# S5 tables, sample step and S5 scan in one row across the borders of the segments, in a hybrid decoder step on Trainium2

## The chip, the cores and the metric

One core of one Trainium2 chip runs the whole program. The metric is device microseconds from start to end of one execution; lower is better. Times before are the median of three runs. The profile is of one further execution.

## What is computed

One layer of a decoder for one prompt of 2048 tokens (width 1024) and 8 sample tokens: a mixer of mLSTM heads, S5 groups and gated-DeltaNet heads, then cross-attention and a SwiGLU FFN. Cut to the part around the change:

```
def mixer_block(x, state, lp):
    z = (rmsnorm(x, lp['norm_mix']) @ lp['w_in']).astype(f32)
    a_q, a_k, a_v, a_o, a_i, a_f, s_u, c_qkv, c_g, c_b, c_a = jnp.split(z, IN_SPLITS, axis=-1)
    ha, c1, n1, m1 = mlstm_chunked(q, k, v, a_i + ..., a_f + ..., c0, n0, m0)
    ys, s5r1, s5i1 = s5_scan(s_u.reshape(B, S, S5_GROUPS, S5_P), s5r0, s5i0, ...)
    gy = jax.nn.gelu(ys.reshape(B, S, S5_WIDTH))
    ys = gy * jax.nn.sigmoid(gy @ lp['s5_w_glu'].astype(f32))
    ...
    hc, S1 = gdn_chunked(gq, gk, gv, beta, log_alpha, S0)
    mix = jnp.concatenate([ha, ys, hc], axis=-1).astype(x.dtype)
    return x + mix @ lp['w_out'], (...)
```

`s5_scan` is a complex diagonal recurrence for 32 groups of 16 channels and 64 states. The kernel turns it into products with matrices built from the powers of each state's factor: that is what its S5 tables are.

## The kernel before

The prompt is cut into four segments of 512 tokens, `sg[0]` to `sg[3]`; the 8 sample tokens ride with the first. `win(s)` (from L443) is the input projection of one segment: 18 GEMMs of 128 output columns over the tokens, each over 8 blocks of the inner dimension with three matmuls a block (the product of two fp32 numbers by their split halves: wh times xh, wh times xl, wl times xh), and then a token-major part with three weights. For `sg[0]` a GEMM has two blocks of columns, 264 and 256. Each result is multiplied by R, the tokens' norm factor spread over the partitions (`norm_b`, copied from PSUM at L384), into a `t` tile on DVE (L152 and L155, the evacuation), and written to DRAM. Between the GEMMs of win(0) stand the 16 memory tiles (`mem_tile`, 256 columns, for the keys and values of cross-attention); between those of win(1) and win(2) eight `fold` steps each. `post(i)` is the rest of a segment: the S5 gate, output projection, cross-attention, FFN.

Weights in win(0) to win(2) come raw: SP loads `wr` (L321, ring of three), ACT casts it to `wh` (L296), POOL subtracts to get `wl` (L152), PE uses both. Raw weights are loaded and split up to two ahead. Rings that matter: `t` five tiles (`tt()`), `acc` one (`acct()`), `big` three, `x` eight, PSUM `P` four and `M` four.

Behind the GEMMs run generators that hold the rest of the mixer: `s5_tables` (from L990), `gates` and `gdn`, `mlstm`, `sample` (from L1382, the sample tokens' step), `s5` (from L1276, the scan, two halves of the prompt). `start(g, rate)` puts one in the list `bg`, `tick(w)` advances each by its rate times w steps (0.5 or 1 per GEMM), `drain` runs it to its end on the spot, `delay(n)` is n empty steps. Before, the tables are drained between win(0) and win(1), the sample step between win(1) and win(2), and scan half 0 at GEMM 17 of win(3). The order on each engine, then, is that of a scheduler that simulates the program written in this order; weights and evacuations have a priority over the generators.

Places that the change touches: `win_sq` (from L419) loads the tokens row by row into eight `t` tiles for a segment (`t<-in_xtok`, L428) and squares them on ACT (L429, sum into `rsq`); `win_rs` makes the norm factor of that with POW on POOL. `s5_tables` has two POW of 48 columns on POOL (L1007), complex powers (E) with temporaries in `t` tiles, sixteen pairs of transposes and small matmuls (L1253, and L164 with `big` and `t` as operands, in the loop over `g0`) whose inputs `bload` takes from DRAM tile T into `t` tiles (`t<-T`). In DVE's rows L1181 is the start of the E powers. `gyd` is the DRAM buffer between the scan, which writes it (L1345), and post, which reads it (`gy_load`, L1691) into a `t` tile for the gate (L1726). 

The table steps and the generator's loop that matter most:

```
        for g0 in range(0, 32, 4):
            nb_ = bload(g0 + 4) if g0 < 28 else None
            ...
                    PE.transpose(P[:, gi * 128:gi * 128 + 128], x, ident)
                    mm(P[:, 256 + gi * 16:272 + gi * 16], x, CC[:, g0 + 2 * hh + gi, :])
```

Of the kernel before, what the change touches and what calls it, by code (L numbers as in the profile page):

```python
# [66 lines left out]
def build(ctx, tc, I, O):  # L67
# [140 lines left out]
    gyd = dtile([2, 512, 8, 128], "gyd")  # L208
# [29 lines left out]
    bg = []  # L238
# [164 lines left out]
    pre = {}  # L403
# [15 lines left out]
    def win_sq(s):  # L419
# [10 lines left out]
        p["col"] = col  # L430

# [313 lines left out]
    def gdn_batch(c0, n):  # L745
# [109 lines left out]
        for j in range(n):  # L855
# [17 lines left out]
            yield  # L873
        nl = n * 16
# [115 lines left out]
    def s5_tables():  # L990
# [11 lines left out]
        def pexp(out, x):  # L1002
# [4 lines left out]
            TT(G, out, eb, x, POW)  # L1007
# [138 lines left out]
        for q0 in (0, 8):  # L1146
            SY.dma_start(pb[0], I["s5b"][:, 0, q0:q0 + 8, :])
            SY.dma_start(pb[1], I["s5b"][:, 1, q0:q0 + 8, :])
            yield from delay(2)
# [24 lines left out]
            yield from delay(2)  # L1174
# [8 lines left out]
            while m < 16:  # L1183
                x1 = tt()[:, 0:8 * m].rearrange("p (q c) -> p q c", q=8)
                x2 = tt()[:, 0:8 * m].rearrange("p (q c) -> p q c", q=8)
# [8 lines left out]
            for a0, an in ((1, 1), (2, 2), (4, 3)):  # L1194
                x1 = tt()[:, 0:8 * an].rearrange("p (q c) -> p q c", q=8)
                x2 = tt()[:, 0:8 * an].rearrange("p (q c) -> p q c", q=8)
# [32 lines left out]
        for a in range(4):  # L1229
            SY.dma_start(t5[a, :, 0:7, :], z[:, 0:7, :])  # L1230
        bb = bt()
# [5 lines left out]

        def bload(g0):
            b = tt()[:, 0:512].rearrange("p (g c) -> p g c", g=4)
            SY.dma_start(b, T1[g0:g0 + 4].rearrange("g n c -> n g c"))  # L1240
            return b

        b = bload(0)
        TS(V, CC[64:128], CC[64:128], -1.0, MUL)
# [20 lines left out]
        for l in range(8):  # L1265
            SY.dma_start(T5[:, :, 7 + l, :].rearrange("g p c -> p g c"), GG[16 * l:16 * l + 16])
        yield
# [8 lines left out]
    def s5(hf):  # L1276
# [50 lines left out]
        def st_b(g, ut, tb, mc, ms, Py):  # L1327
# [15 lines left out]
            for gi in range(2):  # L1343
                f0 = (g - 1 + gi) * 16
                SY.dma_start(gyd[hf, f0:f0 + 16].rearrange("p t c -> t p c"), q[:, gi, :])  # L1345
# [342 lines left out]
    def gy_load(s, i, T):  # L1688
        g_ = tt()
        c0 = (s.i % 2) * 64  # L1690
        SY.dma_start(g_[:, 0:512].rearrange("p (t c) -> p t c", t=8), gyd[s.i // 2, i * 128:(i + 1) * 128, :, c0:c0 + 64])  # L1691
# [359 lines left out]

    def chain(*gs):
        for g in gs:
            yield from g
# [4 lines left out]
    def win_during(s, n0=8, n1=11):  # L2059
        def f(n):  # L2060
            if n == n0:
                win_load(s)
            if n == n1:
                win_sq(s)
            if n == n1 + 2:
# [29 lines left out]
    f1 = win_during(sg[1], 3, 13)  # L2095
    win(sg[0], win0_during, win_after(sg[1]))
    drain(tabs)
    gA = start(chain(gates(0, 4), gdn(sg[0])), RT[1])
    mA = start(chain(delay(3), mlstm(sg[0])), RT[2])
    smp = start(chain(delay(1), sample()), RT[3])  # L2100
# [9 lines left out]
    drain(smp)  # L2110
    s5a = start(s5(0), RT[4])
    win(sg[2], win_fold(8, win_during(sg[3])), win_after(sg[3]))

    def pre0_during(n):
        if n == 17:
# [3 lines left out]
            drain(gA, mA, s5a)  # L2119
# [39 lines left out]
RT = [3.1, 1.6, 0.624, 1.767, 1.05, 1.092, 0.359, 0.972, 0.42, 1.1, 0.4, 1.1, 0.37]  # L2159
# [159 lines left out]
```

## Time and profile before

| | |
|---|---|
| median of 3 runs | 3242.23 us (3241.91 to 3251.68) |
| the profiled execution | 3239.78 us |
| its span, first to last instruction | 3238.0 us |
| busy: PE, DVE, ACT, POOL | 94%, 60%, 27%, 24% of the span |
| mean granted clock of TensorE | 0.973 |
| win(0) from 0, win(1) from 277, win(2) from 470, win(3) from 654, post 0 from 813 us | |

An instruction's row gives its line, engine and operation, the tile it writes and those it reads; L12 is line 12 of the kernel before. A line of a helper (L152, L155 and L164 are the helpers for elementwise work and for matmuls) covers many places, so that tiles tell which. A wait's row says who waited, for whom, and for how long in all.

### The profile page before, as it was taken

The page shows a single profiled execution, that of the slowest core. Times are in us where ns is not written, and L with a number is a line of the kernel's source. Part 1 is how long each engine was busy: PE and PEld are TensorE (multiplying, and loading weights), DVE is VectorE, ACT ScalarE, POOL GpSimd, SP SyncE. Part 2 cuts the span into 40 slices and gives each one's busy share as a digit, 9 for nine tenths or more (in the row PEclk, how much of TensorE's full clock was granted, in tenths as well). Part 3 has the DMA queues.
Part 4 walks back from the last instruction along what each step waited for, and adds up shares of the span by engine and source line. Part 5 has one row for each costly group of instructions (what it writes and reads, how often), then busy time and mean ns, then how long its engine had stood idle before and what let it go on. Part 6 is the DMA issues. An engine that isn't in the chain of part 4 may idle for free.

```text
span 3238.0 us, 49043 instructions
## 1 busy us (share of the span) xinstructions
PE 3045.7 (94%) x18185; PEld 2604.6 (80%) x18185; DVE 1933.2 (60%) x4313; ACT 867.9 (27%) x1761; POOL 772.4 (24%) x572
## 2 busy tenths in 40 slices
PE   7768889999889999999999999999999999999998
PEld 6768768778877777787799999978787787888886
DVE  8744675785789789667755665556445445332224
ACT  3124443532543232234221211132111112210001
POOL 5433545543354444431201100000000000000000
PEclk9888999999999999999999999999999999999999
DMA  7789666766778879786565665665556558455554
GB/s 230 208 205 245 199 197 215 233 205 172 266 244 301 306 260 330 265 283 235 196 211 188 208 220 181 196 236 183 178 177 199 184 174 262 159 195 185 192 183 155
DMA packets 440590, 701.16 MB, mean 217 GB/s; under 512 B 167556, under 2 KB 267628, under 8 KB 440320
## 3 DMA queue, kind: packets, MB, share of 16 engines
q1 hardware_dynamic: 401792, 673.79, 64.4%
q10 hardware_dynamic: 38560, 24.24, 2.8%
q8 instruction: 144, 2.36, 0.3%
q14 instruction: 94, 0.77, 0.1%
HBM read 533.92 MB, written 168.18 MB: 217 GB/s over the span
## 4 chain that ended last, share of the span: by engine, by line
PE 70%; DVE 13%; DMA 8%; issue 5%; POOL 2%; ACT 1%; SPq 1%; ACTq 0%; POOLq 0%; DVEq 0%
PE P L164 62%; PE M L164 7%; DVE big L152 3%; DVE t L155 2%; POOL wl L152 1%; DVE s5h L155 1%; DMA TB<-big 1%; DVE t L152 1%; DVE x L152 1%; DVE TB L152 1%; DMA t<-in_xtok 1%; DMA ABd<-AW 1%; DMA wr<-in_wmq 1%; DVE H L155 0%; DVE x L155 0%
## 5 line engine op out<-in xcount | busy, mean ns | idle before, releaser
L164 PE MATMUL P<-H,wh 128*128 128x512 f32 (+2 forms) x8032 | 2178.4, 359 | 60.4 <-DVE t L152 18.9
L164 PEld LDWEIGHTS P<-H,wh 128*128 128x128 f32 x8032 | 1415.8, 191 | 285.3 <-issue 17.0
L164 PE MATMUL P<-H,wl 128*128 128x512 f32 (+2 forms) x4016 | 1429.7, 357 | 13.1 <-POOL wl L152 12.2
L164 PEld LDWEIGHTS P<-H,wl 128*128 128x128 f32 x4016 | 765.4, 191 | 127.8 <-POOL wl L152 15.4
L152 POOL TENSOR_TENSOR wl<-wr,wh 128x1024 fp32r<-128x1024 f32 (+3 forms) x225 | 541.4, 2411 | 641.4 <-ACT wh L296 560.2
L296 ACT CAST wh<-wr 128x1024 fp32r<-128x1024 f32 (+3 forms) x227 | 231.0, 1021 | 389.7 <-PE P L164 208.9
L152 DVE TENSOR_TENSOR x<-x,P 128x512 f32<-128x512 f32 (+2 forms) x312 | 182.1, 589 | 247.8 <-PE P L164 246.2
L152 DVE TENSOR_TENSOR big<-big,big 32x60 f32<-32x60 f32 (+16 forms) x512 | 238.8, 467 | 29.5 <-DMA big<-ABd 20.5
L164 PE MATMUL P<-wh,H 128*128 128x256 f32 (+1 forms) x1280 | 241.5, 287 | 7.1 <-ACT pp L1799 3.8
L152 DVE TENSOR_TENSOR t<-P,R 128x512 f32<-128x512 f32 (+3 forms) x190 | 115.7, 614 | 218.3 <-PE P L164 180.9
L164 PEld LDWEIGHTS P<-wh,H 128*128 128x128 f32 x1280 | 202.1, 191 | 10.9 <-ACT pp L1799 7.5
L1681 ACT CAST H<-t 128x512 fp32r<-128x512 f32 (+1 forms) x120 | 73.5, 621 | 508.2 <-DVE t L152 491.9
L152 POOL TENSOR_TENSOR rs<-rcol,mhalf 128x4 f32<-128x4 f32 (+2 forms) x17 | 18.8, 1103 | 743.1 <-DVE rcol L161 734.4
L155 DVE SCALAR_TENSOR_TENSOR t<-P,R 128x512 f32<-128x512 f32 (+1 forms) x120 | 69.9, 583 | 210.7 <-PE P L164 206.7
L164 PE MATMUL P<-wl,H 128*128 128x256 f32 (+1 forms) x640 | 181.9, 285 | 1.1 <-DMA wl<-ws_A 0.7
L155 DVE SCALAR_TENSOR_TENSOR t<-t,t 128x512 f32<-128x512 f32 (+3 forms) x140 | 106.4, 765 | 67.1 <-ACT t L1912 41.6
L152 DVE TENSOR_TENSOR H<-t,H 128x512 fp32r<-128x512 f32 (+1 forms) x120 | 90.6, 764 | 64.6 <-ACT H L1681 64.4
L1912 ACT ACTIVATE t<-t 128x512 f32<-128x512 f32 (+1 forms) x88 | 55.7, 633 | 270.7 <-DVE t L152 270.5
L164 PEld LDWEIGHTS P<-wl,H 128*128 128x128 f32 x640 | 122.0, 191 | 2.4 <-DMA wl<-ws_A 1.0
L152 POOL TENSOR_TENSOR ms<-gs,TB 128x128 f32<-128x128 f32 x64 | 32.1, 502 | 356.4 <-ACT Gend L1318 118.3
L155 DVE SCALAR_TENSOR_TENSOR H<-x,VEC,H 128x512 fp32r<-128x512 f32 (+2 forms) x104 | 90.6, 887 | 28.9 <-ACT H L348 26.9
L155 DVE SCALAR_TENSOR_TENSOR t<-g,VEC,t 128x256 f32<-128x256 f32 x144 | 88.7, 616 | 13.3 <-ACT t L760 11.5
(429 smaller groups left out, 2974.5 us busy)
## 6 DMA issues: line engine op xcount, KB each, us to landing
wr<-in_wF SPq DMA_DIRECT2D x72, 512.0 KB
wh<-ws_g SPq DMA_DIRECT2D x66, 512.0 KB
wl<-ws_g SPq DMA_DIRECT2D x66, 512.0 KB
wh<-ws_p SPq DMA_DIRECT2D x66, 512.0 KB
wl<-ws_p SPq DMA_DIRECT2D x66, 512.0 KB
TB<-TB SPq DMA_DIRECT2D x64, 417.0 KB
wh<-ws_d SPq DMA_DIRECT2D x48, 512.0 KB
wl<-ws_d SPq DMA_DIRECT2D x48, 512.0 KB
```

The lines of the kernel that those rows point to most:

```text
L152: eng.tensor_tensor(out=out, in0=a, in1=b, op=op)
L155: V.scalar_tensor_tensor(out=out, in0=a, scalar=s, in1=b, op0=op0, op1=op1, **kw)
L164: PE.matmul(out, l, r, start=st, stop=sp)
L296: S.copy(wh[:, 0:n], raw[:, 0:n])
L1681: S.copy(h[:, 0:T], src[:, 0:T])
L1912: S.activation(th[:, 0:Tb], gt[:, 0:Tb], AF.Tanh, scale=0.5)
```

## The change

1. The drains at both borders go. The tables' rate falls from 3.1 to 2.65, with more delays in them; the sample step starts when the tables are done, scan half 0 when the sample step is done, at rate 1.42 for 1.05, and it is drained with the others at GEMM 17 of win(3). The DeltaNet's triangular solve waits for the tables' end (`after_(hold["tabs"])`).
2. The E powers' temporaries come from an arena in a TB tile, and the inputs of the transposes from the two halves of one `big` tile, not from `t`.
3. The token rows of segments 1 to 3 are loaded one at a time into the one `acc` tile (`win_sq1`), each load at its own GEMM, not eight at once.
4. `gyd` has a block for each segment: a partition's row is read as 2 KB in one run, where it was eight runs of 256 B; the scan writes twice as many pieces, of 256 B a run, where it was 512 B.
5. POOL's POW over 48 columns is cut in six; `win_load` of segments 2 and 3 stands at GEMM 5, not 8.

Core of the diff:

```
-    bg = []
+    bg, hold = [], {}
...
+    def win_sq1(s, i):
+        p = pre[s.i]
+        if i == 0:
+            p["col"] = mt([128, 8], "rcol", 3)
+        if i > 0:
+            q = p["tk"]
+            S.activation(q[:, 0:512], q[:, 0:512], AF.Square, accum_out=p["sq"][:, i - 1:i])
+        if i < 8:
+            p["tk"] = q = acct()
+            t0 = s.x0 + (i // 2) * 128
+            SY.dma_start(q[:, 0:512], I["xtok"][t0:t0 + 128, (i % 2) * 512:(i % 2) * 512 + 512])
...
+        yield from after_(hold["tabs"])
         nl = n * 16
         A = bt()
...
-            TT(G, out, eb, x, POW)
+            for a in range(0, 48, 8):
+                TT(G, out[:, a:a + 8], eb[:, a:a + 8], x[:, a:a + 8], POW)
...
-            yield from delay(2)
+            yield from delay(2 if q0 == 0 else 5)
...
-            yield from delay(2)
+            yield from delay(6)
             er, ei = bt(), bt()
...
-                x1 = tt()[:, 0:8 * m].rearrange("p (q c) -> p q c", q=8)
-                x2 = tt()[:, 0:8 * m].rearrange("p (q c) -> p q c", q=8)
+                x1 = A0([128, 64], "x1")[:, 0:8 * m].rearrange("p (q c) -> p q c", q=8)
+                x2 = A0([128, 64], "x2")[:, 0:8 * m].rearrange("p (q c) -> p q c", q=8)
...
+        yield from delay(5)
         bb = bt()
...
+        b3 = bt()
+
         def bload(g0):
-            b = tt()[:, 0:512].rearrange("p (g c) -> p g c", g=4)
+            o = (g0 // 4 % 2) * 512
+            b = b3[:, o:o + 512].rearrange("p (g c) -> p g c", g=4)
             SY.dma_start(b, T1[g0:g0 + 4].rearrange("g n c -> n g c"))
             return b
 
         b = bload(0)
+        yield from delay(3)
...
-            for gi in range(2):
-                f0 = (g - 1 + gi) * 16
-                SY.dma_start(gyd[hf, f0:f0 + 16].rearrange("p t c -> t p c"), q[:, gi, :])
+            for sg in range(2):
+                for gi in range(2):
+                    f0 = (g - 1 + gi) * 16
+                    SY.dma_start(gyd[2 * hf + sg, f0:f0 + 16].rearrange("p t c -> t p c"),
+                                                     q[:, gi, 64 * sg:64 * sg + 64])
...
-        c0 = (s.i % 2) * 64
-        SY.dma_start(g_[:, 0:512].rearrange("p (t c) -> p t c", t=8), gyd[s.i // 2, i * 128:(i + 1) * 128, :, c0:c0 + 64])
+        SY.dma_start(g_[:, 0:512], gyd[s.i, i * 128:(i + 1) * 128].rearrange("p t c -> p (t c)"))
...
+    def after_(e):
+        while e in bg:
+            yield
+
...
-    def win_during(s, n0=8, n1=11):
+    def win_during(s, n0=8, n1=5):
         def f(n):
-            if n == n0:
+            if n == min(n0, n1):
                 win_load(s)
-            if n == n1:
-                win_sq(s)
-            if n == n1 + 2:
+            if n1 <= n < n1 + 9:
+                win_sq1(s, n - n1)
+            if n == n1 + 9:
                 win_rs(s)
...
-    f1 = win_during(sg[1], 3, 13)
+    f1 = win_during(sg[1], 3, 5)
     win(sg[0], win0_during, win_after(sg[1]))
-    drain(tabs)
+    hold["tabs"] = tabs
     gA = start(chain(gates(0, 4), gdn(sg[0])), RT[1])
     mA = start(chain(delay(3), mlstm(sg[0])), RT[2])
-    smp = start(chain(delay(1), sample()), RT[3])
+    smp = start(chain(after_(tabs), sample()), RT[3])
+    s5a = start(chain(after_(smp), s5(0)), RT[4])
...
-    drain(smp)
-    s5a = start(s5(0), RT[4])
...
-            drain(gA, mA, s5a)
+            drain(gA, mA, smp, s5a)
...
-RT = [3.1, 1.6, 0.624, 1.767, 1.05, 1.092, 0.359, 0.972, 0.42, 1.1, 0.4, 1.1, 0.37]
+RT = [2.65, 1.6, 0.624, 1.75, 1.42, 1.092, 0.359, 0.972, 0.42, 1.1, 0.4, 1.1, 0.37]
```

The scheduler moves more than the diff shows. On ACT, at the copy of R in win(0); `acc` and `t` with `rsq` are the squares of token rows, `wh<-wr` the casts, which PE's next weights need. Before:

```order
L296 CAST wh_574<-wr_354 128x1024
L429 ACTIVATE t_334,rsq_156<-t_334 128x512
L429 ACTIVATE t_337,rsq_156<-t_337 128x512
L429 ACTIVATE t_340,rsq_156<-t_340 128x512
L429 ACTIVATE t_343,rsq_156<-t_343 8x512
L429 ACTIVATE t_346,rsq_156<-t_346 8x512
L296 CAST wh_610<-wr_430 128x1024
L384 COPY R_510<-M_511 128x512
L392 COPY R_510<-M_517 128x8
L296 CAST wh_683<-wr_572 128x1024
```

With the change:

```order
L438 ACTIVATE acc_1280,rsq_940<-acc_1280 128x512
L296 CAST wh_618<-wr_416 128x1024
L438 ACTIVATE acc_1417,rsq_940<-acc_1417 128x512
L438 ACTIVATE acc_1523,rsq_940<-acc_1523 128x512
L438 ACTIVATE acc_1623,rsq_940<-acc_1623 128x512
L384 COPY R_496<-M_497 128x512
L392 COPY R_496<-M_503 128x8
L438 ACTIVATE acc_1736,rsq_940<-acc_1736 128x512
L296 CAST wh_689<-wr_560 128x1024
L296 CAST wh_727<-wr_616 128x1024
L438 ACTIVATE acc_1846,rsq_940<-acc_1846 128x512
L438 ACTIVATE acc_1956,rsq_940<-acc_1956 128x512
```

Three squares of segment 1's rows (1417, 1523, 1623) now stand between one weight's cast and the copy of R, one more ahead of the next cast (689), and two more (1846, 1956) behind it. All 24 squares of segments 1 to 3 stand in win(0), the rest of them about one ahead of each cast; two (1152, 1280) stand further up and one stands behind GEMM 14's cast, so that 21 stand from 1417 to that cast.

On SP, at the same place, the loads behind these squares, with the weights' loads (`wr`) and the memory tiles' writes (`kvd<-t`):

```order
L442 DMA acc_1280<-in_xtok 128x512
L321 DMA wr_560<-in_wmk 128x1024
L1595 DMA kvd<-t_390 128x256
L321 DMA wr_616<-in_wF 128x1024
L1595 DMA kvd<-t_393 128x256
L442 DMA acc_1417<-in_xtok 128x512
L442 DMA acc_1523<-in_xtok 128x512
L442 DMA acc_1623<-in_xtok 128x512
L1241 DMA uf<-TB_281 1024x1x16 x3
L442 DMA acc_1736<-in_xtok 128x512
L321 DMA wr_687<-in_wmk 128x1024
```

Before, there were only the loads of segment 0's rows in this stretch, and SP went on from the second write `kvd<-t` to `uf<-TB` and the next `wr`. Now three `acc` loads stand between, each of which needs the buffer back from the square of the one ahead.

On PE, the tables' transposes (`M<-C`, C being the constants with the identity) and their small matmuls. Before, in GEMM 15 of win(0), among its matmuls (`P<-H,wh`):

```order
L164 MATMUL P_2427<-H_293,wh_2170 128x256
L164 MATMUL M_2081<-big_2041,t_2044 128x16
L1253 MATMUL M_2081<-C,t_2044 128x128
L164 MATMUL M_2081<-big_2041,t_2044 128x16
L164 MATMUL M_2089<-big_2041,t_2044 128x16
L1253 MATMUL M_2089<-C,t_2044 128x128
L164 MATMUL M_2089<-big_2041,t_2044 128x16
L1253 MATMUL M_2101<-C,t_2078 128x128
L164 MATMUL M_2101<-big_2041,t_2078 128x16
L1253 MATMUL M_2101<-C,t_2078 128x128
```

With the change, in GEMM 3 of win(1):

```order
L164 MATMUL P_2823<-H_2569,wl_2727 128x512
L1272 MATMUL M_2873<-C,big_2747 128x128
L164 MATMUL M_2873<-big_2744,big_2747 128x16
L1272 MATMUL M_2873<-C,big_2747 128x128
L164 MATMUL M_2873<-big_2744,big_2747 128x16
L1272 MATMUL M_2881<-C,big_2747 128x128
L164 MATMUL M_2881<-big_2744,big_2747 128x16
L1272 MATMUL M_2881<-C,big_2747 128x128
L164 MATMUL M_2881<-big_2744,big_2747 128x16
```

All 96 of these instructions stand in win(1) now, from GEMM 3 to GEMM 6 with the fold between, and none in win(0) (before: 2 of the transposes and their matmuls in GEMM 13, the most in GEMM 15, the rest in GEMM 17); they read `big` instead of `t`. The sample step's matmuls, which stood dense from GEMM 4 of win(1) to the first of win(2), stand from GEMM 9 of win(1) to GEMM 11 of win(2), and the scan's from GEMM 13 of win(2) to GEMM 17 of win(3) (before: GEMM 4 of win(2) to GEMM 16 of win(3)). On SP the reads `t<-gyd` of post 0 stand right behind the scan's last four writes of `gyd`. On POOL, three of the first POW's pieces stand, then a subtraction `wl`, three more, two subtractions, and then the second POW's six pieces in a row ahead of `rs`.

## Rows read from the trace of the kernel before

**Rows 1.** The page of the profile: busy time; granted clock in 40 slices.
```profile
PE 3045.7 (94%) x18185; PEld 2604.6 (80%) x18185; DVE 1933.2 (60%) x4313; ACT 867.9 (27%) x1761; POOL 772.4 (24%) x572
...
PEclk9888999999999999999999999999999999999999
```

**Rows 2.** Busy time by stretches: us, busy of PE, PEld, DVE, ACT, POOL; clock, DMA share, GB/s.
```profile
56.40:205.10 148.70, 113.50 (x845) 109.74 (x844) 113.86 (x245) 23.81 (x23) 59.63 (x24) 0.91 0.71 196
205.10:277.20 72.10, 56.80 (x433) 56.19 (x434) 23.33 (x32) 30.01 (x87) 18.73 (x10) 0.83 1.03 245
277.20:469.90 192.70, 169.36 (x934) 134.55 (x932) 125.78 (x278) 75.33 (x136) 89.42 (x57) 0.94 0.72 203
469.90:654.30 184.40, 179.79 (x1018) 149.07 (x1018) 120.07 (x313) 87.35 (x195) 98.02 (x89) 0.99 0.74 227
...
3000.00:3050.00 50.00, 50.00 (x217) 40.47 (x216) 15.70 (x23) 5.01 (x8) 0.00 (x0) 1.00 0.57 189
```

**Rows 3.** PE's waits, 200 to 280 us: who waits <- releaser: us, times, longest.
```profile
PE M L1253 <- DMA t<-T: 14.2, 2, 8.5
PE P L164 <- DVE t L152: 6.1, 1, 6.1
```

**Rows 4.** DVE's waits, 200 to 280 us.
```profile
DVE t L152 <- ACT t L429: 17.8, 2, 14.9
```

**Rows 5.** Groups by form, PE, 0 to 277.2 us: busy, mean ns, idle before.
```profile
L1253 PE MATMUL M<-C,t 128*128 128x128 f32 x32 | 10.6, 349 | 14.2 <-DMA t<-T 14.2
L164 PE MATMUL M<-big,t 128*128 128x16 f32 x64 | 10.5, 245 | 0.0
```

**Rows 6.** Timeline of ACT: start, us, instruction, idle before it.
```profile
49.59 0.58 ACT L384 COPY R<-M 128x512 f32<-128x512 f32 x1 [3.81 <-PE M L383]
```

**Rows 7.** Timeline of SP, first memory tile's writes.
```profile
44.72 0.40 SPq L1572 DMA_DIRECT2D kvd<-t  x1
```

**Rows 8.** The chain of waits: start, us, what.
```profile
240.35 4.65 DMA t<-in_xtok
...
596.14 5.78 DMA t<-in_xtok
...
828.57 6.20 DMA t<-gyd
```

**Rows 9.** Groups by form, ACT, 0 to 277.2 us.
```profile
L296 ACT CAST wh<-wr 128x1024 fp32r<-128x1024 f32 x36 | 37.4, 1046 | 150.4 <-DMA TB<-big 39.0 <-PE P L164 33.1 <-DMA wr<-in_wF 20.4
L429 ACT ACTIVATE t<-t 128x512 f32<-128x512 f32 x16 | 10.0, 626 | 9.0 <-DMA t<-in_xtok 8.3 <-ACT big L1259 0.5
```

**Rows 10.** Groups by form, POOL, 0 to 277.2 us.
```profile
L152 POOL TENSOR_TENSOR wl<-wr,wh 128x1024 fp32r<-128x1024 f32 x34 | 85.2, 2516 | 113.2 <-ACT wh L296 108.2 <-PE P L164 5.0
L152 POOL TENSOR_TENSOR big<-big 128x48 f32<-128x48 f32 x2 | 16.5, 8248 | 0.0
```

**Rows 11.** PE's waits, 50 to 200 us.
```profile
PE P L164 <- DVE t L152: 9.9, 4, 4.5
PE M L164 <- ACT wh L296: 8.1, 3, 4.5
PE M L164 <- POOL wl L152: 7.7, 5, 2.3
```

**Rows 12.** DVE's waits, 50 to 200 us.
```profile
DVE big L1181 <- DMA TB<-big: 20.6, 2, 10.7
```

**Rows 13.** PE's waits, 280 to 460 us.
```profile
PE M L164 <- DVE TB L152: 8.0, 3, 3.6
PE M L606 <- DVE TB L152: 3.1, 1, 3.1
```

**Rows 14.** Issues of one tile: ns min/median/max, first and last start.
```profile
L1345 SPq DMA_DIRECT2D gyd<-s x64: 573/600/641, 534.1 to 2054.5; - x64
```

**Rows 15.** Timeline of SP, end of win(3).
```profile
787.41 0.58 SPq L1345 DMA_DIRECT2D gyd<-s  x1
...
801.29 0.57 SPq L1691 DMA_DIRECT2D t<-gyd  x1
```

More of the change, by code (lines that the diff above doesn't have):

```diff
@@ L207, in build @@
     mixd = dtile([4, 128, SEQ + NB], "mixd")
-    gyd = dtile([2, 512, 8, 128], "gyd")
+    gyd = dtile([4, 512, 8, 64], "gyd")
     gys = dtile([512, NB], "gys")
@@ L1194, in s5_tables @@
             for a0, an in ((1, 1), (2, 2), (4, 3)):
-                x1 = tt()[:, 0:8 * an].rearrange("p (q c) -> p q c", q=8)
-                x2 = tt()[:, 0:8 * an].rearrange("p (q c) -> p q c", q=8)
+                x1 = A0([128, 64], "x1")[:, 0:8 * an].rearrange("p (q c) -> p q c", q=8)
+                x2 = A0([128, 64], "x2")[:, 0:8 * an].rearrange("p (q c) -> p q c", q=8)
                 cmul(hi_[0][:, :, a0:a0 + an], hi_[1][:, :, a0:a0 + an], hi_[0][:, :, 0:an], hi_[1][:, :, 0:an],
@@ L1266, in s5_tables @@
             SY.dma_start(T5[:, :, 7 + l, :].rearrange("g p c -> p g c"), GG[16 * l:16 * l + 16])
+            if l % 2 == 1:
+                yield
         yield
@@ L2050, in build @@
         wl_post(i)
+    def after_(e):
+        while e in bg:
+            yield
     def chain(*gs):
```

## The prediction

> **What bounds the kernel now.** I read the page first. PE is busy for 94% of the span [rows 1], so in most of it a change can win nothing but by taking work off PE, and this one takes none off: no GEMM goes, none comes. The reader is to see in the clock line that only slices 2 to 4 (81 us each) lie under 9, so what can be won lies early. I then read busy time by stretch [rows 2], cut at win(0)'s GEMM 2 (56.4 us), its GEMM 14 (205.1), and the starts of win(1), win(2) and win(3). The last of these rows, deep in the FFN, is the measure: 217 matmuls of 512 columns in 50 us, 0.230 us each at full clock. By it, a sample-carrying GEMM (24 matmuls over 520 columns) is worth 5.6 us and a memory tile (24 of 256 columns) 2.8. GEMMs 2 to 13 and their twelve memory tiles are then worth 101 us and take 148.7; GEMMs 14 to 17 and the token-major part (120 matmuls of 272 columns, 14.7 us) are worth 37 and take 72.1; win(1) has 23 us and win(2) 5 in which PE is idle. Third, the waits of these stretches: in the tail of win(0), PE waits 14.2 us for the transposes' t<-T loads and 6.1 for an evacuation into a t tile [rows 3], while DVE's evacuations wait 17.8 us for the squares that hold the t ring [rows 4]. So a ring of five t tiles, shared by evacuations, squares and the table builder, sets the tail.
>
> **The change part by part.** The sum is made against the profiled execution, 3239.8 us, which lies 2.4 under the median of the runs.
>
> *Tail of win(0).* The 32 transposes and their 64 small matmuls [rows 5] leave the tail for win(1), their inputs come out of a big tile, and eight of the t loads at a time are gone. What stays is worth 37 us at full pace, and at the 0.83 clock of that stretch [rows 2] 37/0.83 = 45: **-27**. The ends: only the 14.2 us of rows 3 go (-14), or full pace (-35).
>
> *Start of win(0).* Here the order of ACT tells what the diff doesn't: three squares through the one acc buffer now stand ahead of the copy of R, without which no GEMM of win(0) is evacuated. Before, that copy ran at 49.6 us [rows 6]. The first of the three loads stands on SP behind the second write of the memory tile, which was issued at 44.7 us [rows 7]. One link is a load (4.65 to 5.78 us on the chain [rows 8]) and its square (0.63 [rows 9]), since the next load waits for the buffer: 5.3 to 6.4 us, and three of them end at 61 to 64. So R comes some 12 us later: **+12**. The ends are 0 (were the evacuations late anyway) and +18 (the two further links that stand ahead of the ninth weight's cast not made up).
>
> *Head of win(0).* POOL's two powers over 48 columns take 8.25 us each [rows 10] and are cut into six; a weight's subtraction (2.5 us [rows 10]) may now slip between the first six pieces, but the last six still stand together ahead of rs: 0, between -4 and +2 for the fixed parts. From GEMM 2 to 13 PE waits 25.7 us for DVE, for the casts and for the subtractions [rows 11], and DVE itself waits 20.6 us for the transfers that empty the big tiles [rows 12]. The added delays put the step that waited four ticks later, and the temporaries leave the t ring. I take over half of PE's 25.7: **-14**, between 0 and -26. With the start, the head gives -2.
>
> *Tables in win(1).* Their 96 PE instructions were busy for 21.1 us [rows 5]; there they were strewn over a PE that waited, in win(1) they stand among GEMMs that wait little. Pipelined among other matmuls they cost less than their busy time: **+10**, between +5 and +21. Their copies are on ACT, 39% busy in win(1) [rows 2].
>
> *Sample and scan across borders.* PE's waits for the sample step's DVE work, 8.0 and 3.1 us [rows 13], come from a step that stands dense ahead of its drain; strewn over both segments they should go for the most part: **-9**, between -11 and +5, because the scan now has to fit into fewer GEMMs (rate 1.42 for 1.05), with its last work a GEMM later.
>
> *The gyd buffer.* Reads: one such load stood on the chain with 6.20 us, where a row load of the same 2 KB a partition, the layout that it now gets, stood with 4.65 to 5.78 [rows 8]. One in post 0 and one in post 1, each some 1.4 us shorter: **-3**, between -6 and +6. Writes: 64 more issues of 0.600 us [rows 14], 38 us of SP, which PE doesn't wait for; hidden by weights that are loaded two ahead, up to +4 if that cover is thin. The Trainium skill speaks against these writes: "DMA: Bandwidth & Descriptors", section "Specifications", has 512 B as the least transfer at line rate, below which the engine reads, modifies and writes, and the new runs are 256 B for 512. No row here shows such a write alone. By the rows, the last write was issued 13.9 us ahead of the first read [rows 15]; now the read stands right behind four writes, so a slow write would show as one longer wait, bounded by a whole landing, 6 us [rows 8]: 3217 by the rule, 3211 by the rows, which I take.
>
> Loads of x at GEMM 5 and the Arena temporaries: nothing, DVE's instructions are the same; without that cover the x loads are 8 issues of at most 0.6 us on SP [rows 14].
>
> Sum: -27 - 2 + 10 - 9 - 3 = -31, 3209 against the profiled execution, **3211** against the median.
>
> **The rivals.**
> *It comes back in win(1) and win(2).* DVE and ACT do as much there as before and more: tables, gates and sample in one row. Then the tables cost their whole 21 us instead of 10 and the -9 is lost, and the scan's last steps meet the drain in win(3), with a wait as long as the longest now for DVE there, some 8 us in all: 3211 + 11 + 9 + 8 = 3239. For it: DVE is 65% busy in win(1) and win(2) [rows 2], and the waits of rows 13 are DVE's. Against it: win(2) has PE at 97% with the same kind of work.
>
> *The single buffer sets win(0)'s pace, slower.* The reads were to be one a GEMM over three segments; in the order all 24 stand in win(0), about one ahead of each weight's cast, on SP between the weights' loads. So in this point the change does not do what it says. From 44.7 us on, 21 links stand ahead of GEMM 14's cast; at 5.8 us each they end at 167, well before the time at which that GEMM ran (205.1 [rows 2]), and cost nothing. But SP takes its queue in order, and where the load stands behind a weight that waits for its ring slot or a store that waits for its evacuation, a link grows by up to a weight's time, 4.2 us on average, to 10. Then GEMM 14 comes at 44.7 + 210 + 1.0 (cast [rows 9]) + 2.5 (subtraction) = 258, 53 us late, and the rest of the sum gives back 27 - 10 + 9 + 3 = 29: 3242 + 53 - 29 = 3266. It decides for slower from a link of about 9.3 us on. For it: the first links, as worked out. Against it: ACT is 16% busy there [rows 2], and the mean link has to be twice what its rows give. In the Trainium skill the same page, section "Rules for kernel authors", says to issue a load early and to wait for it late; one buffer does neither, since each load is issued when its predecessor is used up. This case's links of rows 8 are what that leaves exposed.
>
> *The head runs at PE's pace.* With DVE's 20.6 us gone and the links short, GEMMs 2 to 13 lose their whole 25.7 us, R's delay costs 8 of its 12, and the tail goes to full pace: head -18, tail -35, tables +5, borders -11, gyd -3, together -62: 3180. For it: DVE needs 114 us of the 148.7 [rows 2]. Against it: an engine that far loaded rarely delivers without gaps.
>
> **How the numbers follow.** The forecast has 0.54, with its own range 3197 to 3225. The return in win(1) and win(2) 0.17, the slower case 0.12, the head at PE's pace 0.17. The range leaves out the better half of the last and most of the slower one: 3180 to 3250. A measurement of this kernel tells 0.3%, 10 us, from no change. Faster by more (under 3232): forecast and head, 0.71, and a little of the first rival, 0.73. Within: most of the first rival and the mild end of the single buffer, 0.15. Slower: 0.12.
>
> **What would show it.** In the changed profile: R's copy at 61 to 64 us; no PE wait for t<-T, and win(0) from GEMM 14 to its end in 45 us; the transposes at GEMMs 3 to 6 of win(1), with win(1) no more than 10 us longer for them; no long waits for the sample's DVE work at the borders; t<-gyd on the chain with 5 us. It is wrong if win(0) ends later than at 265 us, if PE waits there for wh casts behind squares, or if win(1) and win(2) together take over 385 us (377 now [rows 2]).

## The result and the profile after

The change runs in 3214.0 us (median of 4 runs, 3202.8 to 3215.3) against 3244.1 of the kernel before (4 runs): a ratio of 0.9896, with a 95% interval of 0.9867 to 0.9924. The forecast was 3211. The profiled execution took 3215.3 us; its span is 3213.5, 24.5 less than before.

Where the 24.5 us come from is read by stages. The borders are the first matmuls of GEMM 2 and 14 of win(0), of win(1) to win(3) and of post 0 in the timeline of PE:

| stage | before | after | difference | in the forecast |
|---|---|---|---|---|
| start, to GEMM 2 of win(0) | 56.4 | 61.9 | +5.5 | +12 |
| head, GEMMs 2 to 13 | 148.7 | 135.5 | -13.2 | -14 |
| tail, GEMM 14 to win(1) | 72.1 | 51.4 | -20.7 | -27 |
| win(1) and win(2) | 377.1 | 374.8 | -2.3 | +10 and -9 |
| win(3) | 159.0 | 173.5 | +14.5 | 0 |
| posts 0 to 3 | 2424 | 2416 | -8.3 | -3 |

The sum was met, its terms were not. The busy times of the stages in the changed kernel (the columns of [rows 2]):

```profile
61.90:197.40 135.50, 114.18 (x865) 110.86 (x865) 102.62 (x223) 36.42 (x60) 62.25 (x26) 0.92 0.86 240
197.40:248.80 51.40, 42.90 (x320) 41.77 (x318) 28.70 (x51) 15.02 (x22) 16.04 (x10) 0.93 0.94 229
248.80:441.30 192.50, 171.12 (x1013) 142.39 (x1014) 114.93 (x239) 81.37 (x174) 82.91 (x54) 0.94 0.76 215
441.30:623.60 182.30, 176.52 (x967) 142.56 (x966) 125.73 (x309) 76.63 (x154) 100.30 (x77) 0.99 0.70 205
623.60:797.10 173.50, 163.63 (x964) 136.72 (x964) 116.14 (x344) 52.02 (x129) 72.84 (x75) 0.97 0.68 194
```

Beside [rows 2], PE is busy for 42.9 us of the tail where it was for 56.8, and for 163.6 of win(3), against

```profile
654.30:813.30 159.00, 153.73 (x899) 128.07 (x897) 110.59 (x305) 48.76 (x112) 65.80 (x61) 0.98 0.68 191
```

in the kernel before. So 14 of the tail's 21 us are busy time that left it, and in win(3), where more of the scan now stands, PE is busy for 10 us more. PE's matmuls of the scan with `ut`, by lines, in win(3) of the kernel before:

```profile
L164 PE MATMUL M<-ut,TB 128*128 128x136 f32 (+2 forms) x93 | 14.8, 288 | 1.9 <-DVE s5h L1334 1.9
```

and in win(3) of the changed kernel:

```profile
L164 PE MATMUL M<-ut,TB 128*128 128x136 f32 (+2 forms) x130 | 21.9, 290 | 6.7 <-DVE s5h L1355 4.9 <-DMA TB<-TB 1.8
```

They are 130 for 93. PE's idle time from the start to post 0 fell from 106 to 94 us (the stage's length less its busy PE, summed): of 16 us gained by then, only 11 were PE standing still. The other 5 are less busy time for as many matmuls; the granted clock of the tail is 0.93, where it was 0.83 [rows 2].

PE's waits in the head of the changed kernel (50 to 197 us), which answer to [rows 11]:

```profile
PE M L164 <- POOL wl L152: 8.2, 6, 1.9
PE P L164 <- POOL wl L152: 6.7, 6, 2.7
PE M L383 <- POOL rs L152: 6.4, 1, 6.4
PE M L164 <- ACT wh L296: 4.5, 2, 2.7
```

and DVE's there, to [rows 12]:

```profile
DVE big L1195 <- DMA TB<-big: 22.0, 2, 12.1
```

The 9.9 us for evacuations are gone and the waits for casts and subtractions are hardly longer in all (21.4 us for 19.6, with the smaller rows); the one for `rs`, new in the list, ends at 54 us, ahead of GEMM 2. One more wait went from this stage: of the two for the transposes' loads that the prediction put to the tail [rows 3], the first ended just ahead of GEMM 14 (PE's timeline in the kernel before):

```profile
204.96 0.69 PE L1253 MATMUL M<-C,t 128*128 128x128 f32 x2 [5.72 <-DMA t<-T]
```

The two that went, 9.9 and 5.7 us, less the growth of the others, are the 14 us by which PE's idle time fell in the head (35.2 to 21.3). DVE's wait for the transfers that empty the big tiles is as long as before: 22.0 for 20.6 us (L1195 is L1181 of before). In the tail (197 to 250 us) the waits of [rows 3, 4] have no successor over 2.6 us on PE:

```profile
PE P L164 <- DVE ZS L155: 2.6, 2, 2.1
PE P L164 <- ACT wh L296: 2.2, 1, 2.2
...
PE P L164 <- POOL wl L152: 1.9, 1, 1.9
```

The chain of token rows through the one `acc` tile ran slower than the prediction's sum had it: from the square 1417 (51.4 us) to the last one (198.2) it has 21 links, 7.0 us each on average and up to 13. Most plainly one cast stood behind such a square and its load, and PE waited for both halves of that weight (ACT's timeline, then PE's):

```profile
126.65 0.63 ACT L438 ACTIVATE acc<-acc 128x512 f32<-128x512 f32 x1 [7.28 <-DMA acc<-in_xtok]
...
127.28 1.03 ACT L296 CAST wh<-wr 128x1024 fp32r<-128x1024 f32 x1
```

```profile
128.37 0.51 PE L164 MATMUL P<-H,wh 128*128 128x264 f32 x2 [1.98 <-ACT wh L296]
...
131.54 0.59 PE L164 MATMUL P<-H,wl 128*128 128x264 f32 x1 [2.66 <-POOL wl L152]
```

In win(1) the two waits for the sample step of [rows 13] are there as before, 16.6 us for 11.1 (L1433 is a line of the sample step):

```profile
PE M L164 <- DVE TB L152: 8.4, 1, 8.4
PE M L164 <- DVE TB L1433: 8.2, 2, 6.7
```

At the end of win(3) PE stands 3.4 us for ACT, whose chain of evacuations stands behind a cast that waits for the sample's part of the gate's input, written by the scan's last step (ACT's timeline):

```profile
796.15 0.62 ACT L1704 CAST H<-t 128x520 fp32r<-128x520 f32 x1 [4.60 <-DMA t<-gys]
796.68 0.47 ACT L522 ACTIVATE t<-P,rs 128x256 f32<-128x256 f32 x1
797.05 0.27 ACT L523 ACTIVATE GC<-P,rs 128x16 f32<-128x16 f32 x1
```

### The profile page after: what moved, and what is told of

Same layout as the page of the kernel before. It is cut to its first block, busy times and chain, and to the rows that moved or that the text cites. A ratio compares the mean times of both kernels' runs of the same rounds, so it can differ in the third digit from the quotient of the medians.

```text
span 3213.5 us, 49192 instructions
## 1 busy us (share of the span) xinstructions
PE 3045.0 (95%) x18185; PEld 2606.9 (81%) x18185; DVE 1923.1 (60%) x4313; ACT 867.8 (27%) x1761; POOL 780.2 (24%) x582
## 4 chain that ended last, share of the span: by engine, by line
PE 65%; DVE 7%; DMA 4%; issue 2%; ACT 1%; POOL 1%; SPq 0%; POOLq 0%; ACTq 0%; DVEq 0%
PE P L164 58%; PE M L164 6%; DVE t L155 1%; DVE big L152 1%; DVE s5h L155 1%; DMA wl<-ws_o 1%; DMA wh<-ws_B 1%; POOL wl L152 1%; DMA t<-mixd 0%; DVE x L152 0%; DVE H L155 0%; DVE acc L152 0%; DVE t L152 0%; DVE TB L155 0%; DMA ws_o<-wh 0%
## 5 line engine op out<-in xcount | busy, mean ns | idle before, releaser
L164 PEld LDWEIGHTS P<-H,wl 128*128 128x128 f32 x4016 | 764.1, 190 | 133.2 <-POOL wl L152 21.4
L152 POOL TENSOR_TENSOR wl<-wr,wh 128x1024 fp32r<-128x1024 f32 (+3 forms) x225 | 542.6, 2416 | 615.7 <-ACT wh L296 518.3
L152 DVE TENSOR_TENSOR x<-x,P 128x512 f32<-128x512 f32 (+2 forms) x312 | 182.3, 589 | 244.3 <-PE P L164 220.9
L164 PE MATMUL P<-wh,H 128*128 128x256 f32 (+1 forms) x1280 | 248.2, 291 | 10.0 <-ACT pp L1821 4.2
L152 DVE TENSOR_TENSOR t<-P,R 128x512 f32<-128x512 f32 (+3 forms) x190 | 116.2, 614 | 216.1 <-PE P L164 198.2
L155 DVE SCALAR_TENSOR_TENSOR H<-x,VEC,H 128x512 fp32r<-128x512 f32 (+2 forms) x104 | 96.4, 943 | 16.6 <-ACT H L348 14.9
```

What stands on the lines that cost most here:

```text
L152: eng.tensor_tensor(out=out, in0=a, in1=b, op=op)
L155: V.scalar_tensor_tensor(out=out, in0=a, scalar=s, in1=b, op0=op0, op1=op1, **kw)
L164: PE.matmul(out, l, r, start=st, stop=sp)
```

## The experiments

Each kernel was timed beside the kernel before on the same chip, which lay between 3247.7 and 3251.6 us in these, so that ratios are compared, not medians. The stages, in us, from each profiled execution (tail: GEMM 14 of win(0) to win(1)):

| kernel | ratio (95%) | GEMM 2 at | head | tail | win(1) | win(2) | win(3) | posts |
|---|---|---|---|---|---|---|---|---|
| before | 1 | 56.4 | 148.7 | 72.1 | 193.4 | 183.7 | 159.0 | 2424 |
| change | 0.9896 (0.9867 to 0.9924) | 61.9 | 135.5 | 51.4 | 192.5 | 182.3 | 173.5 | 2416 |
| e11, change again | 0.9902 (0.9888 to 0.9915) | 60.6 | 135.2 | 52.6 | 196.6 | 183.9 | 173.2 | 2413 |
| e1 gyd only | 0.9937 (0.9918 to 0.9955) | 57.3 | 147.5 | 74.0 | 199.5 | 183.3 | 160.5 | 2411 |
| e2 row only | 0.9990 (0.9981 to 1.0000) | 56.5 | 138.5 | 72.9 | 201.8 | 192.6 | 151.7 | 2424 |
| e3 ring (and gyd), drains back | 0.9918 (0.9904 to 0.9932) | 61.0 | 135.9 | 61.9 | 210.2 | 182.2 | 158.1 | 2408 |
| e4 token rows in t | 0.9953 (0.9941 to 0.9965) | 61.0 | 137.8 | 61.3 | 195.4 | 180.8 | 182.6 | 2414 |
| e5 writes on ACT | 0.9995 (0.9984 to 1.0007) | 57.2 | 149.1 | 72.5 | 199.4 | 185.1 | 159.3 | 2425 |
| e6 gyd padded | 0.9957 (0.9941 to 0.9972) | 61.5 | 132.5 | 55.5 | 194.0 | 183.9 | 174.8 | 2428 |
| e7 squares behind R | 0.9906 (0.9889 to 0.9924) | 60.7 | 138.8 | 56.5 | 197.3 | 185.4 | 173.7 | 2412 |
| e8 scan's rate 1.6 | 0.9873 (0.9857 to 0.9890) | 60.5 | 138.5 | 54.1 | 196.0 | 183.6 | 167.3 | 2409 |
| e9 writes and x on POOL | 1.0004 (0.9992 to 1.0016) | 57.0 | 150.3 | 73.9 | 199.1 | 184.1 | 158.1 | 2434 |
| e10 scan 1.6, on POOL | 0.9899 (0.9886 to 0.9913) | 61.7 | 135.8 | 55.5 | 197.0 | 182.9 | 168.4 | 2417 |
| e12 whole GEMMs | 1.0009 (0.9995 to 1.0022) | 56.8 | 147.6 | 74.2 | 193.2 | 184.3 | 161.2 | 2435 |

The same kernel twice (the second and third line) differs by 4 us in win(1); before, e9 and e12, which run the same program up to post 0, differ there by 6, at granted clocks of 0.94, 0.92 and 0.93. One profile doesn't decide on less than that.

**gyd alone (e1).** The gyd hunks of the diff, on the kernel before.

```
-    gyd = dtile([2, 512, 8, 128], "gyd")
+    gyd = dtile([4, 512, 8, 64], "gyd")
...
-        SY.dma_start(g_[:, 0:512].rearrange("p (t c) -> p t c", t=8), gyd[s.i // 2, i * 128:(i + 1) * 128, :, c0:c0 + 64])
+        SY.dma_start(g_[:, 0:512], gyd[s.i, i * 128:(i + 1) * 128].rearrange("p t c -> p (t c)"))
```

> The kernel before with the new layout of gyd alone (a block for each segment, reads of 2 KB runs, writes of 256 B runs). Theory: the layout is what the starts of post 2 and post 3 gained (some 8 us each between the two kernels), with about 2 us in post 0 and post 1: 3244 - 18 = 3226, and nothing changes ahead of win(3). Rival one: those steps come from the rest of the change (another order of SP's queue), so that the layout gives the forecast's 3 us: 3241. Rival two, the rule on runs under 512 B: the doubled, halved writes cost more than the reads give, over 3244.

It gained 0.63% (0.45 to 0.82), some 20 us; in the trace the posts are 13 us shorter, nearly all of it where posts 2 and 3 begin, and the other 7 are not placed. So the smallest term of the forecast is the largest gain of a part tried alone. The Trainium skill's rule on runs under 512 B ("DMA: Bandwidth & Descriptors", section "Specifications"), which spoke against the writes, is not seen in the time here: 128 writes of 256 B runs for 64 of 512 B, and win(3) is 1.5 us longer, less than one profile tells.

**The row alone (e2).** Drains, chaining and rates of the change, on the kernel before; the t ring and gyd as there.

```
-    drain(tabs)
+    hold["tabs"] = tabs
...
-    smp = start(chain(delay(1), sample()), RT[3])
+    smp = start(chain(after_(tabs), sample()), RT[3])
+    s5a = start(chain(after_(smp), s5(0)), RT[4])
...
-    drain(smp)
-    s5a = start(s5(0), RT[4])
```

> The kernel before with the row alone: both drains gone, sample behind the tables, scan behind the sample, the new rates; token rows, temporaries and transposes' inputs still through the t ring, gyd as before. Theory A, the place of the work: the tail of win(0), from its GEMM 14 to win(1), falls from 72 to about 52 us because the transposes leave it, win(3) gets 14 us longer, in all 3244 - 21 + 14 = 3237, or some 6 less with the sample's gain. Theory B, the ring: the tail keeps its waits for t tiles and stays at 65 us or more, and with win(3) longer the kernel is at 3250 or over.

No difference that a measurement tells. What the head gains by the tables' lower rate (10 us) and win(3) gains too (7 us, where both theories had it longer), win(1) and win(2) give back. So win(3) is not longer by the row and the rates alone. But the theories were not told apart. Without the added delays of the tables, which were not taken over, all 32 transposes stand in the tail still (PE's lines, tail), and it is 72.9 us long:

```profile
L1254 PE MATMUL M<-C,t 128*128 128x128 f32 x32 | 11.3, 374 | 0.7 <-ACT big L1260 0.7
```

The row by itself, then, moves nothing out of win(0). The added delays stand in the next kernel, with the ring.

**The ring alone (e3).** The changed kernel, its added delays included, with the drains and rates of before.

```
+    drain(tabs)
...
-    smp = start(chain(after_(tabs), sample()), RT[3])
-    s5a = start(chain(after_(smp), s5(0)), RT[4])
+    smp = start(chain(delay(1), sample()), RT[3])
...
+    drain(smp)
+    s5a = start(s5(0), RT[4])
...
-RT = [2.65, 1.6, 0.624, 1.75, 1.42,
+RT = [3.1, 1.6, 0.624, 1.767, 1.05,
```

> The changed kernel with the drains back at both borders, sample and scan started there, and the rates before; token rows through the acc buffer, arena temporaries, inputs in a big tile and the new gyd stay. Theory A: the transposes stand in the tail of win(0) again, which is 65 to 72 us long, win(3) is back at 159, in all 3214 + 17 - 14 = 3217. Theory B: the tail stays near 51 us without t-ring waits, and with win(3) back at 159 the kernel is at 3214 - 14 = 3200, better than the change itself.

Between the theories: a third of the transposes is left in the tail, which is 61.9 us long, and PE still waits 7.4 us there for their loads, which now come into a big tile.

```profile
L1272 PE MATMUL M<-C,big 128*128 128x128 f32 x10 | 3.2, 330 | 8.2 <-DMA big<-T 7.4 <-ACT big L1278 0.8
```

So the length of the tail follows the transposes in it: 72 to 74 us with all, 62 with a third, 51 to 57 with none where the token rows go through acc. Theory A holds so far, and the loads' wait was not the t ring's alone. win(3) is back at 158, but win(1) takes 210.2: about as many matmuls as in the change (1005 for 1013) kept PE busy for 183.5 us and not 171.1, at a granted clock of 0.89 for 0.94. That the drains at its ends do this is not shown. Against e1 (0.9937), which has the same gyd, all this brings 0.2%, some 6 us, and the row on top of it as much again to the change; in both steps the intervals overlap.

**Token rows in t tiles again (e4).**

```
...
-            if n == min(n0, n1):
+            if n == n0:
                 win_load(s)
-            if n1 <= n < n1 + 9:
-                win_sq1(s, n - n1)
-            if n == n1 + 9:
+            if n == n1:
+                win_sq(s)
+            if n == n1 + 2:
                 win_rs(s)
...
```

> The changed kernel with the token rows of segments 1 to 3 loaded eight at a time into t tiles again, at the GEMMs where they stood (and the x loads at GEMM 8). Theory A: the start gets the 5.5 us back that the squares ahead of R's copy cost (GEMM 2 at 56 us), and the tail stays near 51: 3209. Theory B: evacuations wait for squares in the t ring again, 18 us of DVE in the tail as before, of which half reaches PE: 3214 - 5 + 9 = 3218, and more in the tails of win(1) and win(2).

Slower than both theories: the tail is 10 us longer, as B has it, though no transpose is in it, and GEMM 2 did not come earlier (61.0), against A. But PE's 16 us of waits in this tail are for casts and subtractions, none for an evacuation: 10 are for the two halves of a weight for which ACT's cast and POOL's subtraction stood behind the tables' transfers out of a big tile (`TB<-big`, 14.1 and 15.7 us), 6 for one whose cast stood behind squares that waited for their rows. Win(3) is 9 us longer than with the change; at its end PE stood 12.0 us, where the change has 3.4, for a cast that waited for the sample's part of the gate's input (`t<-gys`):

```profile
PE P L164 <- ACT H L1704: 12.0, 1, 12.0
```

So the token rows through the one acc buffer, the rival by which this change was to get slower, make it some 0.5% faster (0.9953 to 0.9899, the mean of the change's two ratios), if the x loads, which went back with them, are worth nothing.

**Squares behind R's copy (e7).** One element of acc is written from R before the first load.

```
...
+            if late and i == 0:
+                V.tensor_copy(q[:, 0:1], hold["R"][:, 0:1])
...
```

> The changed kernel with the first of segment 1's token row loads made to wait for R (one element of the acc tile is written from R ahead of it, on DVE), so that no square stands ahead of R's copy; each chain of 24 links begins some 25 us later. Theory: the start gets its 5.5 us back (R's copy at 50, GEMM 2 at 56 us for 61.9) and keeps most: 3214 - 4 = 3210. Rival, the single buffer: the chain, begun later, stands ahead of the casts of GEMMs 14 to 17 and eats the 5.5 us and more: 3214 to 3225.

It gained nothing, and GEMM 2 still came at 60.7 us. R's copy moved (ACT's timeline in the changed kernel, with the squares ahead of it):

```profile
51.37 0.63 ACT L438 ACTIVATE acc<-acc 128x512 f32<-128x512 f32 x1 [2.67 <-DMA acc<-in_xtok]
...
54.66 0.63 ACT L438 ACTIVATE acc<-acc 128x512 f32<-128x512 f32 x1 [2.57 <-DMA acc<-in_xtok]
...
58.04 0.64 ACT L438 ACTIVATE acc<-acc 128x512 f32<-128x512 f32 x1 [2.66 <-DMA acc<-in_xtok]
...
58.67 0.57 ACT L384 COPY R<-M 128x512 f32<-128x512 f32 x1
```

and in this kernel:

```profile
54.00 0.59 ACT L384 COPY R<-M 128x512 f32<-128x512 f32 x1 [6.53 <-PE M L383]
```

but PE had other work until GEMM 2. What came late is `rs`: POOL's power in pieces (timeline of POOL, the change) takes 20.2 us for 16.5, and the last six pieces stand ahead of `rs`, 5.5 us later than the 47.4 of before.

```profile
25.53 5.25 POOL L152 TENSOR_TENSOR big<-big 128x8 f32<-128x8 f32 x3
...
33.07 5.29 POOL L152 TENSOR_TENSOR big<-big 128x8 f32<-128x8 f32 x3
...
43.21 9.65 POOL L152 TENSOR_TENSOR big<-big 128x8 f32<-128x8 f32 x6
52.82 1.19 POOL L152 TENSOR_TENSOR rs<-rcol,mhalf 128x5 f32<-128x5 f32 x1
```

Every kernel with the split power has GEMM 2 at 60.5 to 61.9, every one without at 56.4 to 57.3. So the split is taken to cost 4 to 5 us there: e4 and e7 rule the squares out, but no kernel leaves out the split alone, and what it gives was not tried.

**The scan's rate (e8).**

```
-RT = [2.65, 1.6, 0.624, 1.75, 1.42,
+RT = [2.65, 1.6, 0.624, 1.75, 1.6,
```

> The changed kernel with the scan's rate at 1.6 for 1.42: its last step falls three weights earlier, ahead of GEMM 17 of win(3). Theory: of win(3)'s 14 us more, 10 are matmuls of the scan that came over from win(2) and stay, but the 7 at its end (PE held by ACT, which waits for the scan's last results) go: win(3) at 166, 3208. Rival: a denser scan makes PE wait for DVE all through win(3) instead, and nothing is won: 3214.

win(3) is 6 us shorter, 4 of them busy PE; the wait at its end is 0.6 us for 3.4. With 0.9873 it is the fastest kernel of the study: faster than the one before by 1.1% at least, and than the change by 0.2 to 0.3%, which the intervals just allow to be nothing.

**Why gyd helps so much (e5, e6, e9, e12).** In the kernel before PE waits 5.3 us at post 2, and 6.0 at post 3, for the fourth weight of the output projection. The timeline of PE there:

```profile
2142.70 1.22 PE L164 MATMUL P<-H,wh 128*128 128x512 f32 x2 [5.26 <-DMA wh<-ws_o]
```

The wait costs more than its length. With each of the two the granted clock fell to the lower of its two levels (1.2 GHz); over the 7.4 us behind the first it was 0.63 on average, which by an estimate (7.4 us at 0.63 are worth 4.7 at 1.00) loses 2.7 us more. In the changed kernel the start of post 2 (2102 to 2155 us) has 1.00:

```profile
2142.60:2150.00 7.40, 7.11 (x20) 5.21 (x21) 2.68 (x6) 2.06 (x5) 1.60 (x4) 0.63 0.82 324
```

```profile
2102.30:2155.10 52.80, 52.51 (x241) 42.21 (x240) 34.20 (x61) 17.59 (x35) 5.28 (x9) 1.00 0.83 278
```

SP issues the fourth weight's load behind the result's writes and the x loads (SP's timeline, before):

```profile
2136.31 0.33 SPq L293 DMA_DIRECT2D wh<-ws_o  x1
```

In the changed kernel that load stands among the writes, a GEMM earlier (SP's timeline), and PE doesn't wait:

```profile
2115.40 0.33 SPq L293 DMA_DIRECT2D wh<-ws_o  x1
```

First, the writes went to ACT in the kernel before (`S.dma_start` for `SY.dma_start` on `O["yT"]`):

> The kernel before with the writes of the result (out_yT, 8 a segment and 8 more in segment 1) issued by ACT, not SP; gyd as before, reads of 256 B runs. In the kernel before the fourth weight of the output projection stands on SP behind all of these writes at the start of posts 2 and 3, and PE waits 5 to 6 us for it; with the new gyd it stands among them. Theory, the order on SP: with the writes out of SP's way the starts of posts 2 and 3 gain some 5 to 8 us each though the reads are as slow as before: 3247 - 13 = 3234. Rival, the reads: the gain came from the reads' fewer runs, so these starts stay as they are: 3245 or over (ACT gets 40 issues more).

No change. The weight then stood on SP behind seven x loads that waited for the writes. So writes and x loads went to POOL (`G.dma_start`):

> The kernel before with the result's writes and the loads of x at the start of posts 1 to 3 issued by POOL, which has nothing to do there, so that nothing stands between the output projection's weights on SP; gyd as before. The run before this one had only the writes moved, and the weight then stood behind seven x loads that waited for them. Theory, the order on SP: PE's wait of 5 to 6 us for ws_o at posts 2 and 3 goes, and their starts gain up to 8 us each: 3248 - 12 = 3236. Rival, the reads: the weights wait for the 1024-run reads ahead of them in the transfer queue all the same, and it stays at 3245 or over.

Again no change, and here SP had nothing else to do: it stood 15.5 us before that load, for PE.

```profile
SPq L293 <- PE P L164: 19.6, 4, 15.5
```

My theory of SP's order falls. What releases the load is a slot of the weights' ring of three, and the order of PE tells when: before, the last three matmuls of the first three GEMMs (those with the last gate's halves, H_22408 and H_22409) all stand behind the third.

```
L164 MATMUL P_22442<-H_22409,wh_22255 128x512
L164 MATMUL P_22442<-H_22408,wl_22256 128x512
L164 MATMUL P_22480<-H_22409,wh_22362 128x512
L164 MATMUL P_22480<-H_22408,wl_22363 128x512
L164 MATMUL P_22529<-H_22409,wh_22438 128x512
L164 MATMUL P_22529<-H_22408,wl_22439 128x512
L164 MATMUL P_22584<-H_22019,wh_22476 128x512
```

Three weights are held until the third GEMM ends. In the changed kernel the first two GEMMs end before the third begins, so a slot is free one GEMM earlier. Why the last gate's halves come late is to be seen on DVE: before, the last gate's step (`t<-t,t`) stands behind the eight steps of the final norm of the segment before (`x<-x,VEC,R`),

```profile
2123.47 5.45 DVE L155 SCALAR_TENSOR_TENSOR x<-x,VEC,R 128x520 f32<-128x520 f32 x8
2128.85 1.12 DVE L155 SCALAR_TENSOR_TENSOR t<-t,t 128x512 f32<-128x512 f32 x1
```

and in the changed kernel ahead of them, here and in post 3:

```profile
2107.60 2.48 DVE L155 SCALAR_TENSOR_TENSOR t<-t,t 128x512 f32<-128x512 f32 x2 [0.77 <-DMA t<-gyd]
...
2112.48 5.46 DVE L155 SCALAR_TENSOR_TENSOR x<-x,VEC,R 128x520 f32<-128x520 f32 x8 [1.01 <-ACT R L392]
```

To see whether that order hangs on the reads or on the writes, gyd was padded in the changed kernel (72 columns a step, 64 used): writes as in the change, reads in runs of 256 B.

> The changed kernel with gyd's rows padded (72 columns a step for 64): the writes are the same 256 B runs, the reads are 1024 runs of 256 B again. By the order the weights of the output projection stand behind the result's writes again, as before. Both the theory of SP's order and that of the reads' runs: posts 2 and 3 lose 8 us each, 3214 + 14 = 3228. Rival: the writes by segment are what helped, then it stays at 3214; or, if 256 B runs in the writes were harmful, this has no gain left and is at 3231 or over.

The orders of DVE, PE and SP went back to those of before, and with them 0.58% (the change's mean, 0.9899, to 0.9957), 19 us, of which the profile has 12 to 15 in the posts; PE waited 6.1 us again at post 2, and 7.7 at post 3:

```profile
PE P L164 <- DMA wh<-ws_o: 6.1, 1, 6.1
```

The last kernel made the third GEMM wait for the first one's evacuation, on top of e9:

```
+            if dep is not None:
+                V.tensor_copy(P[:, 0:1], dep[:, 0:1])
```

> The kernel of the run with writes and x loads on POOL (gyd as before, 3253), and in posts 2 and 3 the third GEMM of the output projection made to wait for the first one's evacuation (one element, on DVE), so that the last three matmuls of the first and of the second stand ahead of the third and not behind it. In that run SP stood 15.5 us before the fourth weight's load, waiting for PE: in the order of PE the last matmuls of the first three GEMMs all stand behind the third, so that none of the three weight slots comes free before. Theory, PE's order: the fourth load is issued one GEMM earlier, PE's 6 to 7 us at the starts of posts 2 and 3 go for the most part, 3253 - 10 = 3243, and the reads of 256 B runs had nothing to do with it on the chip. Rival, the reads: the last gate's result comes late on the chip too, PE waits for it ahead of the third GEMM instead, and it stays at 3250 or over.

Half an answer. The slot came free earlier: SP issued the load right after the second GEMM. But in post 2 the scheduler put the fourth GEMM ahead of the third, so that this weight was needed at once. SP's timeline:

```profile
2140.61 0.32 SPq L293 DMA_DIRECT2D wh<-ws_o  x1
```

and PE's:

```profile
2146.58 1.22 PE L164 MATMUL P<-H,wh 128*128 128x512 f32 x2 [4.73 <-DMA wh<-ws_o]
```

In post 3 PE's order is that of the change, the fourth GEMM behind the third. There PE stood for the last gate's result after all, whose step on DVE still stands behind the norm, and then 3.1 us for the fourth weight, in all as long as before (5.8 us for 6.0):

```profile
2724.08 1.23 PE L164 MATMUL P<-H,wh 128*128 128x512 f32 x3 [2.70 <-ACT H L1686]
```

So it is shown that the weight's load hangs on its slot and the slot on PE's order, and that PE's order alone does not make the gain. The reading that fits all these runs is the scheduler's order on DVE and PE together: both turn with the shape of the reads (e1 one way, e6 back). That the shorter reads act through these orders alone, and not by landing sooner too, was not shown; at post 2 DVE's steps that waited for a read began 5.0 and 5.7 us behind its issue before, 5.2 and 4.7 us in the changed kernel.

**Both together (e10)**, the rate of e8 and the writes on POOL, and **the change again (e11)**:

> The changed kernel with the scan's rate at 1.6 and the same move of writes and x loads to POOL. If the order on SP alone is what posts 2 and 3 had gained, there is little left: 3208 to 3210. If the writes still hold up other weights, some 3 us more in each of posts 1 to 3: 3200.

> The changed kernel itself beside the two others on one chip: 3214, and 4 us over the same kernel with the scan's rate at 1.6.

POOL's issues brought nothing, rather the posts were 8 us longer than in e8, so e10 is no better than the change. The change itself came out as it had (0.9902 for 0.9896).

## Why the prediction was right, and where it was not

The sum (-31, measured -30 between the medians, -24.5 between the two profiled executions) is right partly by luck: its errors cancel.

- *Tail, -27.* Measured -20.7. The waits went, as argued, though 5.7 of the 14.2 us for `t<-T` had stood in the head. e3 and e4 show that it takes both: the transposes out of the tail, and the token rows out of the t tiles. That the rows act through the t ring is not shown; in e4 PE's waits there were for casts. The size was too large: I took the stretch to PE's pace at its old clock, 45 us; 51.4 is 8.5 us of PE idle above the 42.9 busy.
- *Start, +12.* This step failed. The chain of squares was right in place and wrong in price: R's copy came 9 us later, a link took 3.3 us (squares at 51.4, 54.7 and 58.0) and not 5.3 to 6.4, and PE did not need R then (in e7 it came 4.7 us earlier, GEMM 2 only 1.2). The +5.5 come with POOL's split power, which I had costed at nothing, between -4 and +2.
- *Head, -14.* Measured -13.2, but not by the step given for it: DVE's 20.6 us are still there (22.0). Not half of each of PE's waits went but the whole one for evacuations (9.9), with the 5.7 us for `t<-T` that the tail's term had. e2 has -10 by the tables' lower rate, e3 -13 by ring and delays with the old rate; the two don't add up, and which of PE's waits each takes was not separated.
- *Tables in win(1), +10; borders, -9.* Together -2.3 measured for +1. The tables' matmuls were busy for 18 us in win(1); the sample step's waits did not go, they grew from 11.1 to 16.6 us.
- *win(3), 0.* Missed: +14.5. Ten are PE's work, the scan's matmuls: work that is moved through three segments has to arrive in the last. In e2, where the tables stayed in win(0), win(3) was shorter, so that the tables' delay belongs to it. Some 6 of the 14 go if the scan ends earlier (e8). The first rival had the drain (8 us) in it.
- *gyd, -3.* Mis-sized: -8 to -16 in the posts, 20 us by e1. The step compared one read's landing with another's; the gain was in posts 2 and 3, with another order on DVE and PE and the weights' ring, where the forecast did not look.
- *The single buffer, slower.* It did not decide: PE's waits for casts and subtractions in the head hardly grew (21.4 us for 19.6), and taking the buffer away (e4) made the kernel slower. But it was nearer than the sum had it: 7.0 us a link, for 5.8 there and 9.3 to decide, and the last square ahead of GEMM 14's cast ended at 194 us, 3 ahead of that GEMM and not 38.

What would have shown it wrong: win(0) ended at 248.8, before 265; win(1) and win(2) took 375, under 385. Both bounds held while win(3), for which none was set, took back half the gain. The third sign, PE's waits for casts behind squares, did come, by a few us. Of the signs for it the transposes' place and the end of the `t<-T` waits came; R's copy (58.7 for 61 to 64), the tail (51.4 for 45) and the sample's waits did not.

## What to carry to other kernels

A change of a DMA's shape alters a scheduler's order far from the DMA: compare the orders of every stage that reads it, on all engines, not the transfer alone, and look at what a ring of weights waits for. Work that is moved past a border is paid for where the row ends, so the last stage needs a term of its own. And a total that is met says little: with the terms measured, the largest gain of a part tried alone was the one costed lowest, and a higher rate for the scan gave some 6 us more in the profile.

## What the runs showed of the hardware

A power on POOL over 48 columns takes 8.25 us [rows 10], and in six pieces of 8 columns 1.7 us each (20.2 us for twelve): by an estimate, 3.7 us for ten more pieces, about 0.37 us to start one. A token row's load into the freed acc tile and its square repeat every 3.3 us when SP has nothing ahead of it, against 4.65 to 5.78 for the landing alone that the chain showed [rows 8]. With waits of 5.3 and 6.0 us at posts 2 and 3, in stretches where PE is otherwise busy, the granted clock fell to the lower of its two levels; over the 7.4 us behind the first it was 0.63.
